# Interleaving the two halves of the stationary operands of a two-block network on one core

## The chip, the cores and the metric
One core of a Trainium2 chip runs the whole program in one launch. The metric is the device time of an execution in microseconds (us), the median of three runs.

## The reference
The input is x, 256 positions by 1024 features, fp32. Two blocks of two layers each follow one another, and every matrix product is wanted at fp32 accuracy:

- First block: a gMLP mixer (1024 to 4096 columns, GELU, a spatial product over positions, 2048 back to 1024), a SwiGLU FFN, then banded attention with relative bias, a second SwiGLU FFN and an RMS norm. The FFNs are 1024 to 2 x 2816 and 2816 back to 1024.
- Second block, twice: a mixer of three branches (a depthwise convolution, causal attention, gated linear attention in chunks of 32) with an output projection of 1024 rows, then an FFN whose up projection passes through a causal convolution of width 3 before the gate.

```python
def _swiglu_ffn(x, g_norm, w_gate_up, w_down):
    h = _rms_norm(x, g_norm)
    gate, up = jnp.split(h @ w_gate_up, 2, axis=-1)
    return (jax.nn.silu(gate) * up) @ w_down
...
        u = causal_depthwise_conv(h @ ffn_w_up[l].astype(h.dtype), ffn_conv_w[l], ffn_conv_b[l])
        x = x + (jax.nn.silu(u[..., :D_FF]) * u[..., D_FF:]) @ ffn_w_down[l].astype(x.dtype)
```

## The kernel before
Every fp32 operand of a large product is split in two fp32r tiles: a high part `hi` (ScalarE copies the value to fp32r) and a remainder `lo` (VectorE subtracts `hi` from the value). A product is then three matmuls: hi x hi, hi x lo and lo x hi. For activations `split2` does this (L232 on ScalarE, L233 on VectorE), for weights the class `Stream`.

`Stream` brings 406 weight pieces of 128 x 1024 from HBM, two to a DMA of 1 MB (issued by SyncE, three raw buffers), in the order in which the program uses them. `_hi` (L105) and `_lo` (L116, or L118 where a row gain is folded in) split a piece into the tiles `wh` and `wl`, 8 buffers each (`LOOK`), or `xh` and `xl`, 4 buffers (`DEFER`), for the last pieces of an FFN's down projection. `pump` is called at points that are written out by hand between the products and does one such step ahead of need; `take` hands pieces over, `release` gives their buffers back. All instructions stand in program order on their engines.

Four forms of product use the pieces. In a matmul, `lhsT` is the stationary operand: a weight load (LDWEIGHTS, 128 columns) puts it into the array before `rhs`, the moving operand, streams through. Each matmul here loads its own.
- `mmA` (L339): position-major; the stationary operand is a 128-position slice of the normalised activations `hT`, the weights move (512 columns).
- `mmB` (L350 to L352): feature-major; the weight piece is stationary in eight parts of 128 columns, `hT` moves (256 positions), three matmuls a part.
- `mmB_wide` (L363, L366): the same with `hT`'s halves side by side, so that `wide` moves 512 columns under the weight's high part and `low` moves 256 under its remainder. The FFNs' up projections use it.
- `down` (L393 to L395): the activations (`ah`, `al`; `uvh`, `uvl` in the gMLP; `yT` in the mixers, which the profile calls hT) are stationary, the weights move (512 columns).

An FFN loops over 22 feature pairs i: two `mmB_wide`, the gating of pair i (`finish`: in the convolution FFNs L634 to L661, with four three-operand VectorE instructions at L651), and `down` for pair i - 3, which takes four matmul groups of three. The pieces that `mmB` and `mmB_wide` take come from `colsB` in the packing code, those of `mmA` from `colsA`, those of `down` from `rowsK`.

Of the kernel before, what the change touches and what calls it, by code (L numbers as in the profile page):

```python
# [9 lines left out]
F32R = mybir.dt.float32r  # L10
# [5 lines left out]
P = 128  # L16
S = 256
D = 1024
KD = D // P
# [3 lines left out]
LOOK = 8  # L23
NBIG = 12
RAW = 3
DEFER = 4
# [21 lines left out]
class Stream:  # L48

    def __init__(self, nc, raw_pool, pool, units):
        self.nc, self.raw_pool, self.pool = nc, raw_pool, pool
        self.units = units
        self.raw = {}
        self.split = {}
        self.index = []
        for u, (src, ext) in enumerate(units):
            for j, e in enumerate(ext):
                self.index.append((u, j, j == len(ext) - 1, e))  # L60
        self.next_dma = 0
        self.nh = 0
        self.nl = 0
        self.used = 0
        self.order = [[i for i, p in enumerate(self.index) if p[3] == e] for e in (False, True)]
        self.ext_pool = None
        self.ext_left = 0
        self.row_gain = {}

    def dma(self, parts=1, between=None):  # L70
        u = self.next_dma
        if u >= len(self.units):
            return
        src, ext = self.units[u]
        t = self.raw_pool.tile([P, 2048], F32, tag="raw", name="raw")
        n = len(ext) * 1024 // parts
        for i in range(parts):
            self.nc.sync.dma_start(t[:, i * n : (i + 1) * n], src[:, i * n : (i + 1) * n])
            if i == 0 and between is not None:
                between()  # L80
        self.raw[u] = t
        self.next_dma += 1
# [4 lines left out]
    def _hi(self):  # L87
        if self.nh >= len(self.index):
            return False
        u, j, last, e = self.index[self.nh]  # L90
        if e:
            if self.ext_pool is None or not self.ext_left:
                return False
            self.ext_left -= 1
            p, a, b, n = self.ext_pool, "xh", "xl", DEFER
        else:
            if self.used >= LOOK:
                return False
            self.used += 1
            p, a, b, n = self.pool, "wh", "wl", LOOK  # L100
        hi = p.tile([P, 1024], F32R, tag=a, name=a, bufs=n)
        lo = p.tile([P, 1024], F32R, tag=b, name=b, bufs=n)
        r = self.raw[u][:, j * 1024 : (j + 1) * 1024]
        g = self.row_gain.get(self.nh)
        self.nc.scalar.activation(hi, r, AF.Copy, scale=1.0 if g is None else g)  # L105
        self.split[self.nh] = (hi, lo)
        self.nh += 1
        return True

    def _lo(self):  # L110
        u, j, last, e = self.index[self.nl]
        hi, lo = self.split[self.nl]
        r = self.raw[u][:, j * 1024 : (j + 1) * 1024]
        g = self.row_gain.get(self.nl)
        if g is None:
            self.nc.vector.tensor_sub(lo, r, hi.bitcast(F32))  # L116
        else:
            self.nc.vector.scalar_tensor_tensor(lo, r, g, hi.bitcast(F32),  # L118
                                                op0=ALU.mult, op1=ALU.subtract)
        self.nl += 1  # L120
        if last:
            del self.raw[u]
            self.dma()
# [27 lines left out]
class Net:  # L151
# [304 lines left out]
    def gmlp(self, start, hT, half_in, warm, rest, rstd):  # L456
        nc = self.nc
        with self.tc.tile_pool(name="gm", bufs=1) as pool:
# [108 lines left out]
            def group(g):  # L567
                if g % 2 == 0:
                    vnorm(g // 2)
                ps = self.mmB2(hT)  # L570
                u = pool.tile([P, 2, S], F32, tag="u", name="u", bufs=2)
                nc.vector.tensor_mul(u, ps, rrow[:, None, :].to_broadcast([P, 2, S]))
                nc.scalar.activation(u, u, AF.Gelu)
                sp = self.mm([P, 2, 2, P], "sp")
                for j in range(2):
                    f = slice((2 * g + j) * P, (2 * g + j + 1) * P)
                    for t in range(2):
                        nc.tensor.matmul(sp[:, j, t, :], lhsT=v[t][:, f], rhs=wsT[:, g, :],  # L578
                                         start=True, stop=True)
                b = brow[:, g * P : (g + 1) * P]  # L580
                vs = pool.tile([P, 4, P], F32, tag="vs", name="vs", bufs=2)
                nc.vector.tensor_add(vs, sp.rearrange("p j t n -> p (j t) n"),
                                     b[:, None, :].to_broadcast([P, 4, P]))
                nc.vector.tensor_mul(u, u, vs.rearrange("p (j t) n -> p j (t n)", j=2))
                uv = tuple(
                    pool.tile([P, 2, S], F32R, tag=n, name=n, bufs=4) for n in ("uvh", "uvl")
                )
                self.split2(uv[0], uv[1], u)
                uvs[g] = uv

# [29 lines left out]
    def ffn(self, hT, fin, next_gains, conv=None, final=False):  # L620
        nc = self.nc
        with self.tc.tile_pool(name="ff", bufs=1) as pool:
# [5 lines left out]
            def finish(i, ps):  # L628


                if isinstance(ps, list):
                    raw = pool.tile([P, 2, S], F32, tag="sum", name="sum", bufs=2)
                    for j in range(2):
                        nc.scalar.activation(raw[:, j, :], ps[j][:, 1, :], AF.Copy)  # L634
                    for j in range(2):
                        nc.vector.tensor_add(raw[:, j, :], ps[j][:, 0, :], raw[:, j, :])  # L636
                    ps = raw
                if conv is None:
                    g, u = ps[:, 0, :], ps[:, 1, :]
                else:  # L640
                    gu = pool.tile([P, 2, S], F32, tag="gu", name="gu", bufs=2)
                    ws3 = []
                    for j in range(2):
                        q = C_FCV + (conv * 44 + j * NPAIR + i) * 4
                        w = [self.prm[:, q + n : q + n + 1] for n in range(4)]
                        nc.scalar.activation(gu[:, j, :], ps[:, j, :], AF.Identity,  # L646
                                             bias=w[3], scale=w[2])
                        ws3.append(w)
                    for d in (1, 2):
                        for j in range(2):  # L650
                            nc.vector.scalar_tensor_tensor(  # L651
                                gu[:, j, d:], ps[:, j, : S - d], ws3[j][2 - d], gu[:, j, d:],
                                op0=ALU.mult, op1=ALU.add,
                            )
                    g, u = gu[:, 0, :], gu[:, 1, :]
                if conv is None:
                    sg = pool.tile([P, S], F32, tag="sg", name="sg", bufs=2)
                else:
                    sg = g
                nc.scalar.activation(sg, g, AF.Silu)  # L660
                nc.vector.tensor_mul(sg, sg, u)  # L661
                act = tuple(
                    pool.tile([P, S], F32R, tag=n, name=n, bufs=7) for n in ("ah", "al")
                )
                self.split2(act[0], act[1], sg)
                acts[i] = act

# [121 lines left out]
    def attention(self, hTs, fin, second, next_gains):  # L789
        nc = self.nc  # L790
        hkv, hq = hTs
        with self.tc.tile_pool(name="at", bufs=1) as pool:
# [35 lines left out]
            def pv(s):  # L828
                pTs = pTss.pop(s)
                po = self.mm([P, S], "po")  # L830
                for j in range(2):
                    for e in range(2):
                        c = slice((2 * s + e) * 64, (2 * s + e + 1) * 64)
                        r = slice(64 * e, 64 * e + 64)
                        nc.tensor.matmul(po[r, j * P :], lhsT=v[j][:, c],  # L835
                                         rhs=pTs[e][:, 2 * j : 2 + j, :], start=j == 0, stop=j == 1)
                act = tuple(
                    pool.tile([P, S], F32R, tag=n, name=n, bufs=8) for n in ("ah", "al")
                )
                self.split2(act[0], act[1], po)  # L840
                acts[s] = act

# [56 lines left out]
    def mixer(self, l, hT, fin, next_gains):  # L899
# [5 lines left out]
        with self.tc.tile_pool(name="mx", bufs=1) as pool:  # L905
# [312 lines left out]
                nc.vector.tensor_scalar(rsc[:, q], ssc[:, q], 4e-6, None, op0=ALU.add)  # L1218
                self.pow(rsc[:, q], rsc[:, q], 4)

            yT = self.new_hT()

            def b_trans():
                ps = self.mm([P, 2, S], "tr")
# [131 lines left out]
    Net(ctx, tc, a, out, units).run()  # L1356


def _pack(inputs):

    import numpy as np
# [6 lines left out]
        return [t[:, i] for i in range(4)]  # L1368

    def colsB(w):  # L1370
        return [w.reshape(KD, P, P).transpose(1, 0, 2).reshape(P, 1024)]

    def rowsK(w):
        return [w[i * P : (i + 1) * P] for i in range(w.shape[0] // P)]
# [2 lines left out]

    def add(name, pieces, ext=()):
        n = len(pieces)
        if n % 2:  # L1380
            pieces = pieces + [pieces[-1]]
        w = np.stack(pieces).reshape(len(pieces) // 2, 2, P, 1024).transpose(0, 2, 1, 3)
        arr[name] = np.ascontiguousarray(w).reshape(len(pieces) // 2, P, 2048)
        for u in range(len(pieces) // 2):
            plan.append((name, u, [i in ext for i in (2 * u, 2 * u + 1) if i < n]))

    w_in, w_out = f["a_w_in"][0], f["a_w_out"][0]
    ps = []
# [113 lines left out]
```

## Time and profile before
| | |
|---|---|
| median of 3 runs | 1240.5 us (1240.06 to 1240.7) |
| the profiled execution: its time, its span | 1240.27 us, 1238.5 us |
| PE busy, share of the span | 1228.8 us, 99% |
| PEld (weight loads) busy | 1055.0 us, 85% |
| DVE (VectorE) busy | 903.5 us, 73% |
| ACT (ScalarE) busy | 715.1 us, 58% |
| HBM traffic | 226 MB, mean 183 GB/s |

How to read it: busy time of an engine is the union of its instructions. Matmuls are pipelined, so a matmul's own duration is longer than the distance from its start to the next one's start; the page's chain of work follows the last instruction back to what released each step. A group's row has its line, engine and operation, out<-in by the program's names, shapes, the count, then busy us, mean ns of one, and the idle time before with what ended it. L12 is line 12 of the kernel.

### The profile page before, as it was taken

Reading aid. Unit: us, or ns where it says so; the run is one execution under the profiler, and the core shown is the slowest. Engines: PE = TensorE matmul, PEld = TensorE weight load, DVE = VectorE, ACT = ScalarE, POOL = GpSimd, SP = SyncE. Lnnn points to the kernel's source line nnn. Section 1 sums busy time; section 2 is a strip of 40 time slices with the busy share of each in tenths; the row PEclk is TensorE's granted clock in tenths of the full one; section 3 lists DMA queues with packets and bytes.
Section 4 is the critical chain, followed back from the end, with each engine's and each line's share of the span. In section 5 each row is a group of like instructions: output and inputs, shape, how many; then the busy total and the mean of one; then the engine's idle time right before and its main releaser. Section 6 shows DMA issues by size and latency. Waiting matters only on the chain.

```text
span 1238.5 us, 18456 instructions
## 1 busy us (share of the span) xinstructions
PE 1228.8 (99%) x7160; PEld 1055.0 (85%) x7160; DVE 903.5 (73%) x1497; ACT 715.1 (58%) x1237; POOL 41.3 (3%) x95
## 2 busy tenths in 40 slices
PE   9999999999999999999999999999999999999997
PEld 7899888888888888888889878888888978888886
DVE  6676676766567757676669867979885977889874
ACT  7644465655456546565546556667663745767653
POOL 1100000000000000000010010000001011000000
PEclk9999999999999999999999999999999999999999
DMA  8854465675444435567524345557542425566720
GB/s 290 307 201 170 153 210 199 209 267 192 148 161 171 163 134 206 183 238 246 184 103 170 120 155 203 171 187 278 198 170 86 164 75 216 182 221 216 252 71 34
DMA packets 34827, 226.14 MB, mean 183 GB/s; under 512 B 4242, under 2 KB 4660, under 8 KB 9140
## 3 DMA queue, kind: packets, MB, share of 16 engines
q1 hardware_dynamic: 34596, 224.97, 51.7%
q8 instruction: 56, 0.92, 0.3%
q14 instruction: 31, 0.25, 0.1%
q10 hardware_dynamic: 144, 0.00, 0.0%
HBM read 223.91 MB, written 1.05 MB: 182 GB/s over the span
## 4 chain that ended last, share of the span: by engine, by line
PE 97%; DVE 2%; ACT 1%; POOL 0%; issue 0%; POOLq 0%; ACTq 0%
PE mm L363 24%; PE mm L339 12%; PE mm L366 12%; PE acc L393 9%; PE acc L395 9%; PE acc L394 9%; PE mm L350 5%; PE mm L351 4%; PE mm L352 4%; PE tr L239 1%; PE sc L746 1%; PE mm L497 1%; PE pt L777 1%; PE sp L578 1%; PE po L835 1%; PE po L1202 0%
## 5 line engine op out<-in xcount | busy, mean ns | idle before, releaser
L116 DVE TENSOR_TENSOR wl<-raw,wh 128x1024 fp32r<-128x1024 f32 x378 | 458.8, 1223 | 201.0 <-ACT wh L105 200.1
L105 ACT ACTIVATE wh<-raw 128x1024 fp32r<-128x1024 f32 x378 | 395.1, 1055 | 246.1 <-PE mm L363 89.5
L363 PE MATMUL mm<-hT,wh 128*128 128x512 f32 x1280 | 452.1, 397 | 0.0
L366 PE MATMUL mm<-hT,wl 128*128 128x256 f32 x1280 | 333.2, 281 | 0.0
L363 PEld LDWEIGHTS mm<-hT,wh 128*128 128x128 f32 x1280 | 235.2, 188 | 46.2
L366 PEld LDWEIGHTS mm<-hT,wl 128*128 128x128 f32 x1280 | 241.6, 189 | 14.2
L339 PE MATMUL mm<-wh,hT 128*128 128x512 f32 (+1 forms) x480 | 149.1, 383 | 0.0
L350 PE MATMUL mm<-hT,wh 128*128 128x256 f32 x448 | 128.9, 288 | 0.0
L351 PE MATMUL mm<-hT,wh 128*128 128x256 f32 x448 | 126.8, 283 | 0.1
L352 PE MATMUL mm<-hT,wl 128*128 128x256 f32 x448 | 126.6, 283 | 0.0
L393 PE MATMUL acc<-wh,ah 128*128 128x512 f32 x320 | 125.6, 393 | 0.0
L395 PE MATMUL acc<-wh,al 128*128 128x512 f32 x320 | 124.5, 389 | 0.0
L394 PE MATMUL acc<-wl,ah 128*128 128x512 f32 x320 | 124.5, 389 | 0.0
L339 PEld LDWEIGHTS mm<-wh,hT 128*128 128x128 f32 x480 | 86.8, 188 | 16.8 <-issue 1.1
L350 PEld LDWEIGHTS mm<-hT,wh 128*128 128x128 f32 x448 | 85.7, 191 | 5.5 <-issue 5.2
L339 PE MATMUL mm<-wl,hT 128*128 128x512 f32 (+1 forms) x240 | 90.2, 381 | 0.0
L351 PEld LDWEIGHTS mm<-hT,wh 128*128 128x128 f32 x448 | 85.8, 192 | 0.7 <-DVE hT L233 0.5
L352 PEld LDWEIGHTS mm<-hT,wl 128*128 128x128 f32 x448 | 85.8, 191 | 0.0
L636 DVE TENSOR_TENSOR sum<-mm,sum 128x256 f32<-128x256 f32 x160 | 66.6, 419 | 15.1 <-ACT sum L634 15.0
L651 DVE SCALAR_TENSOR_TENSOR gu<-sum,prm,gu 128x255 f32<-128x255 f32 (+1 forms) x160 | 72.7, 480 | 5.4 <-ACT gu L646 3.5
L634 ACT ACTIVATE sum<-mm 128x256 f32<-128x256 f32 x160 | 58.8, 369 | 31.1 <-PE mm L363 30.7
L394 PEld LDWEIGHTS acc<-wl,ah 128*128 128x128 f32 x320 | 60.2, 188 | 13.0
(221 smaller groups left out, 1458.5 us busy)
## 6 DMA issues: line engine op xcount, KB each, us to landing
raw<-in_w_ffn SPq DMA_DIRECT2D x66, 1024.0 KB, 4.9
raw<-in_w_up SPq DMA_DIRECT2D x66, 1024.0 KB, 4.9
raw<-in_w_mix SPq DMA_DIRECT2D x30, 1024.0 KB, 4.9
raw<-in_w_gmlp SPq DMA_DIRECT2D x22, 1024.0 KB, 5.1
raw<-in_w_att SPq DMA_DIRECT2D x16, 1024.0 KB, 4.9
raw<-in_w_gmlp SPq DMA_DIRECT2D x4, 512.0 KB, 6.2
bias<-in_rel SPq DMA_DIRECT2D x8, 256.0 KB, 3.9
x<-in_x SPq DMA_DIRECT2D x4, 256.0 KB, 5.4
```

The lines of the kernel that those rows point to most:

```text
L105: self.nc.scalar.activation(hi, r, AF.Copy, scale=1.0 if g is None else g)
L116: self.nc.vector.tensor_sub(lo, r, hi.bitcast(F32))
L339: mm(out, lhsT=hT[a][:, k, ts], rhs=view(b, k), start=(i == 0), stop=(i == 3 * KD - 1))
L350: mm(out, lhsT=vh[:, k, :], rhs=hT[0][:, k, :], start=(k == 0), stop=False)
L351: mm(out, lhsT=vh[:, k, :], rhs=hT[1][:, k, :], start=False, stop=False)
L352: mm(out, lhsT=vl[:, k, :], rhs=hT[0][:, k, :], start=False, stop=(k == KD - 1))
L363: mm(ps, lhsT=vh[:, k, :], rhs=hT[2][:, k], start=(k == 0), stop=(k == KD - 1))
L366: mm(ps[:, 0, :], lhsT=vl[:, k, :], rhs=hT[0][:, k, :], start=False, stop=False)
L393: mm(acc, lhsT=act[0][:, ts], rhs=w[0][:, c], start=(first and i == 0), stop=False)
L394: mm(acc, lhsT=act[0][:, ts], rhs=w[1][:, c], start=False, stop=False)
L395: mm(acc, lhsT=act[1][:, ts], rhs=w[0][:, c], start=False, stop=(last and i == n - 1))
L651: nc.vector.scalar_tensor_tensor(gu[:, j, d:], ps[:, j, : S - d], ws3[j][2 - d], gu[:, j, d:], op0=ALU.mult, op1=ALU.add,)
```

## The change
The high part and the remainder of operands that are loaded as stationary ones now share one tile and alternate element by element: element n of `hi` lies at 2n, element n of `lo` at 2n + 1. That holds for the weight pieces of `mmB` and `mmB_wide` (marked by a class `Stationary` in `colsB`), and for the activations that `down` takes: `ah`/`al` of FFNs and attention, `uvh`/`uvl`, and the mixers' `yT`. Pieces whose weights move (`colsA`, `rowsK`) share one tile too, but as two runs of 1024, one behind the other. A tile of the stream is 2056 elements of which 2048 are used; before, hi and lo were two tiles of 1024. `hT` of the normalised activations stays as it was. Instructions, their order and the DMAs are the same; the access patterns change: ScalarE writes `hi`, VectorE reads `hi` and writes `lo`, and the weight loads read, all at every second element.

```diff
@@ Stream._hi
-            p, a, b, n = self.ext_pool, "xh", "xl", DEFER
+            t = self.ext_pool.tile([P, 2048], F32R, tag="x", name="x", bufs=DEFER)
...
-            p, a, b, n = self.pool, "wh", "wl", LOOK
-        hi = p.tile([P, 1024], F32R, tag=a, name=a, bufs=n)
-        lo = p.tile([P, 1024], F32R, tag=b, name=b, bufs=n)
+            t = self.pool.tile([P, 2056], F32R, tag="w", name="w", bufs=LOOK)[:, :2048]
+        if inter:
+            t = t.rearrange("p (n j) -> p j n", j=2)
+        else:
+            t = t.rearrange("p (j n) -> p j n", j=2)
+        hi, lo = t[:, 0, :], t[:, 1, :]
@@ gmlp
-                uv = tuple(
-                    pool.tile([P, 2, S], F32R, tag=n, name=n, bufs=4) for n in ("uvh", "uvl")
-                )
+                uv = pool.tile([P, 2, S, 2], F32R, tag="uv", name="uv", bufs=4)
+                uv = (uv[:, :, :, 0], uv[:, :, :, 1])
@@ ffn (attention the same, with 8 buffers)
-                act = tuple(
-                    pool.tile([P, S], F32R, tag=n, name=n, bufs=7) for n in ("ah", "al")
-                )
+                act = pool.tile([P, S, 2], F32R, tag="a", name="a", bufs=7)
+                act = (act[:, :, 0], act[:, :, 1])
@@ mixer
-            yT = self.new_hT()
+            yT = self.hpool.tile([P, KD, S, 2], F32R, tag="hT", name="yT")
+            yT = (yT[:, :, :, 0], yT[:, :, :, 1])
@@ packing
+class Stationary(tuple):
+    def __new__(cls, piece):
+        return super().__new__(cls, (piece,))
...
-        return [w.reshape(KD, P, P).transpose(1, 0, 2).reshape(P, 1024)]
+        return [Stationary(w.reshape(KD, P, P).transpose(1, 0, 2).reshape(P, 1024))]
```

## Rows read from the trace of the kernel before
**Rows 1.** The page: busy us and share, granted clock in 40 slices, chain by engine.
```profile
PE 1228.8 (99%) x7160; PEld 1055.0 (85%) x7160; DVE 903.5 (73%) x1497; ACT 715.1 (58%) x1237; POOL 41.3 (3%) x95
...
PEclk9999999999999999999999999999999999999999
...
PE 97%; DVE 2%; ACT 1%; POOL 0%; issue 0%; POOLq 0%; ACTq 0%
```
**Rows 2.** Waits of PE, then of ACT: us in total, times, longest us.
```profile
PE warm L423 <- POOL ident masks.py:199: 1.4, 1, 1.4
...
PE acc L393 <- ACT ah L232: 0.2, 1, 0.2
...
ACT wh L105 <- PE mm L363: 89.5, 76, 1.8
```
**Rows 3.** Groups by line and shape, whole span.
```profile
L363 PE MATMUL mm<-hT,wh 128*128 128x512 f32 x1280 | 452.1, 397 | 0.0
...
L366 PE MATMUL mm<-hT,wl 128*128 128x256 f32 x1280 | 333.2, 281 | 0.0
...
L350 PE MATMUL mm<-hT,wh 128*128 128x256 f32 x448 | 128.9, 288 | 0.0
...
L393 PE MATMUL acc<-wh,ah 128*128 128x512 f32 x320 | 125.6, 393 | 0.0
...
L393 PE MATMUL acc<-wh,uvh 128*128 128x512 f32 x64 | 25.7, 402 | 0.0
L393 PE MATMUL acc<-wh,hT 128*128 128x512 f32 x64 | 25.5, 398 | 0.0
...
L393 PE MATMUL acc<-xh,ah 128*128 128x512 f32 x60 | 24.1, 402 | 0.2 <-ACT ah L232 0.2
```
**Rows 4.** Timeline of PE in an FFN, 301.2 to 306.3: start us, us.
```profile
301.21 0.40 PE L393 MATMUL acc<-wh,ah 128*128 128x512 f32 x1
...
303.93 0.39 PE L363 MATMUL mm<-hT,wh 128*128 128x512 f32 x1
...
304.27 0.40 PE L363 MATMUL mm<-hT,wh 128*128 128x512 f32 x1
...
304.98 0.40 PE L363 MATMUL mm<-hT,wh 128*128 128x512 f32 x1
305.22 0.28 PE L366 MATMUL mm<-hT,wl 128*128 128x256 f32 x1
305.33 0.40 PE L363 MATMUL mm<-hT,wh 128*128 128x512 f32 x1
...
306.04 0.40 PE L363 MATMUL mm<-hT,wh 128*128 128x512 f32 x1
```
**Rows 5.** Timeline of PE, then of PEld, in a mixer, 694.9 to 699.0.
```profile
694.90 0.28 PE L350 MATMUL mm<-hT,wh 128*128 128x256 f32 x1
...
697.66 0.28 PE L352 MATMUL mm<-hT,wl 128*128 128x256 f32 x1
...
697.68 1.34 PEld L777 LDWEIGHTS pt<-ident,z 128*128 128x128 f32 x12
698.98 0.19 PEld L339 LDWEIGHTS mm<-wh,hT 128*128 128x128 f32 x1
```
**Rows 6.** The chain in order of time, gMLP: start us, us, what.
```profile
59.88 0.89 PE sp L578 x8
```
**Rows 7.** Windows, convolution FFNs: stretch, us, busy of PE, PEld, DVE, ACT, POOL.
```profile
752.00:925.00 173.00, 173.00 (x915) 147.95 (x914) 146.20 (x242) 116.07 (x197) 0.86 (x2) 1.00 0.61 209
1050.00:1225.00 175.00, 174.79 (x922) 149.07 (x921) 142.04 (x240) 110.49 (x190) 0.00 (x0) 1.00 0.49 171
```
**Rows 8.** Groups by line and shape on DVE, whole span.
```profile
L116 DVE TENSOR_TENSOR wl<-raw,wh 128x1024 fp32r<-128x1024 f32 x378 | 458.8, 1223 | 201.0 <-ACT wh L105 200.1
...
L651 DVE SCALAR_TENSOR_TENSOR gu<-sum,prm,gu 128x255 f32<-128x255 f32 x80 | 37.4, 478 | 3.6 <-ACT gu L646 3.5
...
L233 DVE TENSOR_TENSOR al<-sg,ah 128x256 fp32r<-128x256 f32 x44 | 18.5, 420 | 0.3 <-ACT ah L232 0.3
```

More of the change, by code (lines that the diff above doesn't have):

```diff
@@ L57, in __init__ @@
         self.index = []
-        for u, (src, ext) in enumerate(units):
+        for u, (src, ext, kinds) in enumerate(units):
             for j, e in enumerate(ext):
-                self.index.append((u, j, j == len(ext) - 1, e))
+                self.index.append((u, j, j == len(ext) - 1, e, kinds[j]))
         self.next_dma = 0
@@ L73, in dma @@
             return
-        src, ext = self.units[u]
+        src, ext, _ = self.units[u]
         t = self.raw_pool.tile([P, 2048], F32, tag="raw", name="raw")
@@ L89, in _hi @@
             return False
-        u, j, last, e = self.index[self.nh]
+        u, j, last, e, inter = self.index[self.nh]
         if e:
@@ L110, in _lo @@
     def _lo(self):
-        u, j, last, e = self.index[self.nl]
+        u, j, last, e, _ = self.index[self.nl]
         hi, lo = self.split[self.nl]
@@ L836, in pv @@
                                          rhs=pTs[e][:, 2 * j : 2 + j, :], start=j == 0, stop=j == 1)
-                act = tuple(
-                    pool.tile([P, S], F32R, tag=n, name=n, bufs=8) for n in ("ah", "al")
-                )
+                act = pool.tile([P, S, 2], F32R, tag="a", name="a", bufs=8)
+                act = (act[:, :, 0], act[:, :, 1])
                 self.split2(act[0], act[1], po)
@@ L1379, in add @@
         n = len(pieces)
+        kinds = [isinstance(p, Stationary) for p in pieces]
+        pieces = [p[0] if k else p for p, k in zip(pieces, kinds)]
         if n % 2:
@@ L1384, in add @@
         for u in range(len(pieces) // 2):
-            plan.append((name, u, [i in ext for i in (2 * u, 2 * u + 1) if i < n]))
+            plan.append((name, u, [i in ext for i in (2 * u, 2 * u + 1) if i < n], kinds[2 * u : 2 * u + 2]))
     w_in, w_out = f["a_w_in"][0], f["a_w_out"][0]
@@ L1496 @@
     out = nc.dram_tensor("out", (1, S, D), F32, kind="ExternalOutput").ap()
-    units = [(a[name][u], ext) for name, u, ext in plan]
+    units = [(a[name][u], ext, kinds) for name, u, ext, kinds in plan]
     with _tile.TileContext(nc) as tc:
```

## Prediction, made before the changed kernel was run
> **What bounds the kernel now.** Read the page's busy times and its chain first. [...] Then the waits of PE: the longest total is 1.4 us, at the start, and a down projection waits for an activation once, for 0.2 us [rows 2]. So no feeding engine sets the time. What can change it is the time from one matmul's start to the next one's, and the diff changes how the operand that every matmul loads first is laid out. That interval is not the duration in the groups (397 ns for a 512-wide matmul [rows 3]), since matmuls overlap; it is read from the starts in the timeline.
>
> [...]
> - Down projection (L393 to L395, 512 wide): from 301.21 to 303.93 us lie twelve intervals, 2.72 us, 226.7 ns each, 13.3 over the stream [rows 4].
> - Wide pair (L363 with 512 columns, L366 with 256): from 304.98 to 306.04 lie three pairs, 1.06 us, 353.3 ns a pair, 33.3 over the 320.0 of its two streams [rows 4].
> - Narrow triple (L350 to L352, 256 wide): from 694.90 to 697.66 lie 23 intervals, 2.76 us, 120.0 ns each, 13.3 over [rows 5].
>
> So there is time between matmuls that is neither stream nor wait. It is not one constant: the first wide pair after a down projection takes 340 ns (303.93 to 304.27), the settled ones 353 [rows 4], with the same operations on the same kinds of tiles. I read this as two read streams (the load of the next stationary operand, the moving columns of the current one) that get in each other's way by an amount that depends on how they fall against each other. That reading is argued; the rows only show that the amount varies.
>
> How much there is: 1280 pairs at 33.3 ns are 42.7 us; 448 triples, 1344 matmuls, at 13.3 are 17.9; the L393 groups of 512 columns are 320 + 64 + 64 + 60 = 508 [rows 3], as many stand in L394 and L395, and 1524 at 13.3 are 20.3. Together **81 us** over the streams, all in matmuls whose stationary operand the diff lays out anew. The other product, mmA (L339), loads hT, which stays as it is.
>
> **The change part by part.** *The loads.* Each still takes 128 columns of 128 rows, but its elements lie 8 bytes apart instead of 4. No row shows such a load, so bounds from both sides. For the gain, the rows with the closest loads: the transposes load every 108 ns (from 697.68 to 698.98 twelve loads [rows 5]), and the gMLP's spatial matmuls (L578), which load without transposing, start every 111 ns (0.89 us for 8 [rows 6]), that is 4.6 ns over a stream of 106.7. If every stationary operand came down to 4.6 over, a pair gains 24.1 ns, the others 8.7: 1280 x 24.1 + 1344 x 8.7 + 1524 x 8.7 = 30.8 + 11.7 + 13.3 = 56 us. By the transposes' 1.7 it would be 72 us; at nothing left, 81. For the loss: a load is covered by the interval of the matmul before it, 120 ns in the triple and 0.11 us behind the narrow half of a pair [rows 4]; its own pace is 108. So a load that slows by a few per cent costs nothing, and one that doubles (216 ns) raises each interval behind a 256-wide stream to 216: 96 x 1344 + 106 x 1280 = 265 us. I take the gain of 56, by the row that loads in the same manner. The reason for the sign: a contiguous load fetches its bytes at half the pace at which the moving stream does (128 columns in 108 ns, against 256 in 106.7), so the two slide past each other; at 8 bytes a column they advance alike, and an offset found once should last.
>
> *The writers.* ACT's L105 and L232 write, and DVE's L116 and L233 read one and write one operand, at every second element. 216 of the 406 weight pieces are concerned (gmlp 16, four FFNs 40 each, attention 16, mixers 12 each). The instruction counts don't change, and hT's writers are left alone but for the mixers' yT. Below, the price is nothing: these run at one element at a time, 1223 ns for 1024 [rows 8]. Above, the dearest elementwise row: L651, 478 ns for 255 columns, 1.87 ns a column against L116's 1.19 [rows 8], so 0.70 us more a piece and 0.17 more a 256-column activation. I take nothing, since nothing says that a strided operand is like L651. What covers it is DVE's idle time, and that differs by stage: in the loops of the two convolution FFNs DVE is busy 288.2 of 348.0 us, 83% [rows 7].
>
> [...]
>
> *One tile instead of two, padded by 8 elements.* The slot of a weight piece comes free when its last reader is done; hi's last reader and lo's are at most one matmul apart (120 to 227 ns), and ACT waits for such slots already (89.5 us in 76 waits behind L363 alone [rows 2]) without PE waiting. Nothing. Should hi's readers now also wait for the lo written beside it (420 ns [rows 8]), that shows only where a down projection follows its activation at once, in the tails: some 2 us in all, not counted. DMAs, queues and their order don't change.
>
> *The sum.* A loop of a convolution FFN has 16 pairs and 12 down matmuls: 16 x 353.3 + 12 x 226.7 = 8.37 us, DVE at 83% of it 6.93. Its gain is 16 x 24.1 + 12 x 8.7 = 0.49 us, which leaves 7.88 and DVE at 88%. With 348 / 8.37 = 41.6 loops that is 20 us, and I count half of it, because at 88% ACT and DVE, which wait for each other, will let PE wait at times. 56 - 10 = 46. From the profiled execution's 1240.3 us (the median of the runs is 1240.5): **1194 us**.
>
> **Rivals.** *One: DVE becomes the bound in the convolution FFNs.* Two strided pieces and an activation a loop, 2 x 0.70 + 0.17 = 1.57 us, put DVE at 8.50: the 20 us are lost, 0.13 x 41.6 = 5 more are paid, and the other stages keep 36: 1240 + 5 - 36 = 1209. If half of DVE's present idle time (0.72 of 1.44 us a loop, spent waiting for ACT) stays, a loop takes 9.22, 35 us more in all, and the time is 1239. If PE gains nothing as well, the two ends are 1245 and 1275. [...] For it speaks DVE's 83%; against it that L116 already runs at one element at a time.
>
> *Two: the stride makes no difference to TensorE* and its 13 ns are a fixed cost of switching the stationary operand. The exact repeat of 226.7 and 120.0, both 13.3 over, speaks for it; 340 against 353 for the same pair against it. 1240.
>
> *Three, the other side: the loads get slower.* Place: every matmul behind a 256-wide stream, in 1344 + 1280 cases; it decides from a load of 110 to 120 ns on. At 135 ns (a quarter more) the triples pay 15 x 1344 = 20 us and the pairs 25 x 1280 = 32: 1292. At double the time it is 1505; if not the load but the mutual hindrance doubles, 1240 + 81 = 1321. For it: twice as many bytes are spanned by each load. Against it: the load's own 108 ns look like one column at a time, which a stride need not touch.
>
> **How the numbers follow.** Forecast 0.47 (its own range 1168, by the transposes' floor, to 1215); rival one with a gain on PE 0.15 (1209 to 1239, of which 0.02 falls within 0.2%), without one 0.09 (1245 to 1275); rival two 0.14; rival three 0.15. Faster by over 0.2% (about what a measurement of this kernel can tell from no change): 0.47 + 0.13 = 0.60. Same 0.14 + 0.02 = 0.16. Slower 0.09 + 0.15 = 0.24. The range goes from 1168 to 1262, which leaves out rival three and the upper part of rival one without a gain, 0.18 in all.
>
> **What would show it.** In the profile after: wide pairs at about 329 ns, triples at 111, down projections at 218, mmA at its old interval. L116 at 1223 ns for the strided pieces; a second, longer form of it would be rival one, with PE waiting behind DVE in L651 or L363. Loads of over 188 ns in their records and triples over 120 would be rival three. Unchanged intervals would be rival two. Most likely to make me wrong: that the hindrance is not a matter of pace, or that only some of the eight buffers, which the pad shifts by 8 elements each, fall well.

## The result, and the profile after

| | before | after |
|---|---|---|
| median of 4 runs each, us | 1240.34 | 1251.66 |
| lowest to highest, us | 1240.06 to 1240.70 | 1251.58 to 1251.73 |
| ratio, 95% interval | | 1.0091 [1.0074, 1.0109] |
| profiled execution: span, us | 1238.5 | 1249.8 |

The change makes the kernel 11.3 us slower. That lies inside the range that was given (1168 to 1262) and on the other side of the forecast, which was a gain of 46 us. The range was wide enough to take in two rivals, and that the time lies in it is luck.

The page of after, busy time and chain, and the first waits of PE (us in total, times, longest us), answer to [rows 1, 2]:

```profile
PE 1240.3 (99%) x7160; PEld 1078.0 (86%) x7160; DVE 905.9 (72%) x1497; ACT 734.1 (59%) x1237; POOL 42.3 (3%) x95
...
PEclk9999999999999999999999999999999999999999
...
PE 97%; DVE 1%; ACT 1%; issue 0%; POOL 0%; POOLq 0%; ACTq 0%
```
```profile
PE warm L427 <- POOL ident masks.py:199: 1.4, 1, 1.4
PE mm L501 <- DVE w L120: 0.8, 2, 0.4
```

The reader is to see that nothing new is waited for. The 0.8 us behind a weight's remainder stood in the kernel before too. PE is busy 11.5 us longer in a span that is 11.3 us longer, the chain is still PE's for 97%, and the granted clock is 0.999 of full speed, as before. So no feeding engine took the time; it lies between one matmul's start and the next.

The groups of after, by line and shape (busy us, mean ns of one), answer to [rows 3, 8]. Lines are four higher than before: L363 is now L367, L116 is L120, L339 is L343.

```profile
L120 DVE TENSOR_TENSOR w<-raw,w 128x1024 fp32r<-128x1024 f32 x378 | 459.1, 1224 | 210.7 <-ACT w L109 209.1
L109 ACT ACTIVATE w<-raw 128x1024 fp32r<-128x1024 f32 x378 | 413.8, 1105 | 236.8 <-PE mm L367 87.7 <-PE acc L399 64.9 <-PE mm L356 36.1
...
L367 PEld LDWEIGHTS mm<-hT,w 128*128 128x128 f32 x1280 | 244.4, 196 | 39.1
```

The last two of them in the kernel before:

```profile
L105 ACT ACTIVATE wh<-raw 128x1024 fp32r<-128x1024 f32 x378 | 395.1, 1055 | 246.1 <-PE mm L363 89.5 <-PE acc L395 62.5 <-PE mm L351 46.0
...
L363 PEld LDWEIGHTS mm<-hT,wh 128*128 128x128 f32 x1280 | 235.2, 188 | 46.2
```

DVE takes 1224 ns for a weight's remainder (1223 before) and 420 for an activation's (420 before), so the 8-byte step costs it nothing. ACT's high parts rise from a mean of 1055 to 1105 ns, with about half of them written at the step, and ACT is busy 59%. A load of a pair is recorded at 196 ns instead of 188.

The timeline of PE in an FFN (start us, duration us), two loops one after the other, answers to [rows 4]:

```profile
304.38 0.39 PE L397 MATMUL acc<-w,a 128*128 128x512 f32 x1
...
307.15 0.39 PE L367 MATMUL mm<-hT,w 128*128 128x512 f32 x1
...
307.85 0.39 PE L367 MATMUL mm<-hT,w 128*128 128x512 f32 x1
...
308.90 0.39 PE L367 MATMUL mm<-hT,w 128*128 128x512 f32 x1
...
312.76 0.39 PE L397 MATMUL acc<-w,a 128*128 128x512 f32 x1
...
315.57 0.40 PE L367 MATMUL mm<-hT,w 128*128 128x512 f32 x1
```

The twelve intervals of the down projection take 2.77 us in the first loop and 2.81 in the next, about 231 and 234 ns each, against 226.7 in [rows 4]. Three pairs take 1.05 us, 350 ns a pair against 353. So the pairs are hardly changed, the down projection is slower, and no longer by one number. Over the loops that follow each other the means of twelve are 233.5, 233.8, 232.7, 233.1, 234.7, 233.4, 230.2, 230.8, and then the same eight again: they follow the eight weight buffers, which the pad sets 32 bytes apart.

mmA pays too, though its stationary operand was left alone. This is its first long stretch in the chain in order of time (start us, us, what), in the kernel before and then in after:

```profile
20.67 33.01 PE mm L339 x144
```
```profile
20.82 33.61 PE mm L343 x144
```

33.61 instead of 33.01 us for 144 matmuls, 4.2 ns more each. mmA's moving columns are the contiguous weight pieces, and these lie in the same padded ring of buffers.

From the starts in the two traces every interval can be taken. The table gives the mean over the stream: from start to next start, less 213.3 ns at 512 columns and 106.7 at 256. These two are estimates: 106.7 is the difference of the 226.7 ns at 512 columns and the 120.0 at 256 in [rows 4, 5], and 213.3 is twice that. Intervals more than 40 ns over, which hold waits and changes of sequence, are left out of it (16.2 us in all before, 15.9 after); the counts are those of after.

| product, columns | matmuls | before, ns | after, ns | change, us |
|---|---|---|---|---|
| down projection, 512 | 1490 | 14.20 | 19.35 | +7.7 |
| mmA, 512 | 571 | 14.78 | 19.06 | +2.5 |
| pair, narrow half, 256 | 1280 | 10.58 | 11.75 | +1.5 |
| triple, 256 | 1301 | 13.14 | 13.61 | +0.6 |
| pair, wide half, 512 | 1276 | 21.36 | 20.72 | -0.8 |

The sum is 11.5 us. (Five more of mmA's intervals are counted after than before; they are 0.1 of its 2.5.) The same measure, "over" for short, is used for all runs below.

### The profile page after: what moved, and what is told of

It is laid out like the page before. It is cut to its first block, busy times and chain, and to the rows that moved or that the text cites. A ratio compares the mean times of both kernels' runs of the same rounds, so it can differ in the third digit from the quotient of the medians.

```text
span 1249.8 us, 18447 instructions
## 1 busy us (share of the span) xinstructions
PE 1240.3 (99%) x7160; PEld 1078.0 (86%) x7160; DVE 905.9 (72%) x1497; ACT 734.1 (59%) x1237; POOL 42.3 (3%) x95
## 3 DMA queue, kind: packets, MB, share of 16 engines
HBM read 223.91 MB, written 1.05 MB: 180 GB/s over the span
## 4 chain that ended last, share of the span: by engine, by line
PE 97%; DVE 1%; ACT 1%; issue 0%; POOL 0%; POOLq 0%; ACTq 0%
PE mm L367 24%; PE mm L343 12%; PE mm L370 12%; PE acc L397 9%; PE acc L399 9%; PE acc L398 9%; PE mm L354 5%; PE mm L355 4%; PE mm L356 4%; PE tr L243 1%; PE sc L748 1%; PE mm L501 1%; PE pt L779 1%; PE sp L582 1%; PE po L837 1%; PE po L1203 0%
## 5 line engine op out<-in xcount | busy, mean ns | idle before, releaser
L120 DVE TENSOR_TENSOR w<-raw,w 128x1024 fp32r<-128x1024 f32 x378 | 459.1, 1224 | 210.7 <-ACT w L109 209.1
L109 ACT ACTIVATE w<-raw 128x1024 fp32r<-128x1024 f32 x378 | 413.8, 1105 | 236.8 <-PE mm L367 87.7
L367 PE MATMUL mm<-hT,w 128*128 128x512 f32 x1280 | 452.2, 396 | 0.0
L370 PE MATMUL mm<-hT,w 128*128 128x256 f32 x1280 | 334.2, 281 | 0.0
L367 PEld LDWEIGHTS mm<-hT,w 128*128 128x128 f32 x1280 | 244.4, 196 | 39.1
L370 PEld LDWEIGHTS mm<-hT,w 128*128 128x128 f32 x1280 | 250.7, 196 | 11.9
L343 PE MATMUL mm<-w,hT 128*128 128x512 f32 (+1 forms) x720 | 168.9, 386 | 0.0
L343 PEld LDWEIGHTS mm<-w,hT 128*128 128x128 f32 x720 | 126.4, 188 | 27.8 <-issue 2.2
L354 PE MATMUL mm<-hT,w 128*128 128x256 f32 x448 | 129.3, 289 | 0.0
L355 PE MATMUL mm<-hT,w 128*128 128x256 f32 x448 | 127.0, 284 | 0.1
L356 PE MATMUL mm<-hT,w 128*128 128x256 f32 x448 | 126.8, 283 | 0.0
L397 PE MATMUL acc<-w,a 128*128 128x512 f32 x320 | 126.7, 396 | 0.0
L399 PE MATMUL acc<-w,a 128*128 128x512 f32 x320 | 126.3, 395 | 0.0
L398 PE MATMUL acc<-w,a 128*128 128x512 f32 x320 | 126.2, 394 | 0.0
L354 PEld LDWEIGHTS mm<-hT,w 128*128 128x128 f32 x448 | 87.9, 196 | 5.5 <-issue 5.2
L355 PEld LDWEIGHTS mm<-hT,w 128*128 128x128 f32 x448 | 87.9, 196 | 0.7 <-DVE hT L237 0.5
L356 PEld LDWEIGHTS mm<-hT,w 128*128 128x128 f32 x448 | 87.9, 196 | 0.0
L639 DVE TENSOR_TENSOR sum<-mm,sum 128x256 f32<-128x256 f32 x160 | 66.9, 419 | 15.9 <-ACT sum L637 15.6
L399 PEld LDWEIGHTS acc<-w,a 128*128 128x128 f32 x320 | 62.5, 195 | 12.0
L398 PEld LDWEIGHTS acc<-w,a 128*128 128x128 f32 x320 | 62.4, 195 | 11.7
```

The costliest lines, as they stand in the source:

```text
L343: mm(out, lhsT=hT[a][:, k, ts], rhs=view(b, k), start=(i == 0), stop=(i == 3 * KD - 1))
L354: mm(out, lhsT=vh[:, k, :], rhs=hT[0][:, k, :], start=(k == 0), stop=False)
L355: mm(out, lhsT=vh[:, k, :], rhs=hT[1][:, k, :], start=False, stop=False)
L356: mm(out, lhsT=vl[:, k, :], rhs=hT[0][:, k, :], start=False, stop=(k == KD - 1))
L367: mm(ps, lhsT=vh[:, k, :], rhs=hT[2][:, k], start=(k == 0), stop=(k == KD - 1))
L370: mm(ps[:, 0, :], lhsT=vl[:, k, :], rhs=hT[0][:, k, :], start=False, stop=False)
```

## Experiments

**Which part of the change costs.** Theory 1: the pad puts the weights of the eight buffers at offsets that meet the other stream less well. Its rival: a load at a step of 8 bytes is dearer by itself. Five kernels take the change apart. (The theories are numbered as in the expectations; there is none with the number 2.)

*e1_no_pad*: all is interleaved, the pad is gone.
```
-            t = self.pool.tile([P, 2056], F32R, tag="w", name="w", bufs=LOOK)[:, :2048]
+            t = self.pool.tile([P, 2048], F32R, tag="w", name="w", bufs=LOOK)
```


> The changed kernel with weight tiles of 2048 elements instead of 2056, so that all eight start at the same offset within 256 bytes; everything stays interleaved. Theory 1 (the pad puts the moving weights of down and mmA at offsets 32 bytes apart, and their settled interval of 226.7 ns is lost): down back to about 13 to 14 ns over its stream from 19.4, mmA from 19.1 to about 15, time about 1241 us. Rival (the strided loads, 196 ns instead of 188, cost it): intervals as after the change, 1251 us.

*e2_one_tile*: one tile for both parts, as two contiguous runs; no pad, nothing interleaved.
```
-            t = self.pool.tile([P, 2056], ...)[:, :2048]
-        if inter:
+            t = self.pool.tile([P, 2048], ...)
+        if False:
...
-                act = pool.tile([P, S, 2], F32R, tag="a", name="a", bufs=7)
-                act = (act[:, :, 0], act[:, :, 1])
+                act = tuple(pool.tile([P, S], F32R, tag=n, name=n, bufs=7) for n in ("ah", "al"))
```


> Only the joint tile of hi and lo, as two runs of 1024, no pad and nothing interleaved. Theory 1 and the rival alike: 1240 us, as before the change. If it is near 1250 instead, what costs is that hi and lo of a piece lie 4096 bytes apart or share a slot.

*e3_pad_only*: e2 with the tile of 2056.

> The joint tile with the pad of 8 elements, as two runs, nothing interleaved. Theory 1: down about 19 ns over its stream, mmA about 19, time 1249 to 1252 us, with loads at 188 ns. Rival: 1240 us.

*e4_weights_only*: the change with the activations' lines (act, uv, yT) as they were before.

> The changed kernel with the activations of down back in separate contiguous tiles; weight pieces interleaved and padded as in the change. Theory 1: 1249 to 1252 us, down as slow as after the change although its loads are contiguous again. Rival: most of the loss sits in down, so about 1242 to 1243 us.

*e5_acts_only*: e2 with only those activations interleaved; no pad.

> Only the activations of down interleaved; weight pieces in one tile as two runs, no pad. Theory 3 (what costs is the position of the load's reads against the moving reads: a stride of 8 bytes spoils a settled pair of aligned contiguous operands, a pad of 32 bytes does so too): down about 21 ns over its stream as without the pad but all interleaved, nothing else moves, so 1240.3 + 1489 x 7.2 ns = 1251 us. Rival (the strided loads of the weight pieces cost as well): about 1246 us, the rest of the loss being theirs.

Measured, with e8_weights_no_pad, which came later (below) and completes the scheme:

| run | interleaved | pad | us | ratio [95%] | down | mmA | triple | pair (wide + narrow) |
|---|---|---|---|---|---|---|---|---|
| before | nothing | no | 1240.34 | | 14.20 | 14.78 | 13.14 | 21.36 + 10.58 |
| e2 | nothing, one tile | no | 1240.31 | 0.9999 [0.9991, 1.0008] | 14.16 | 14.83 | 13.14 | 21.38 + 10.56 |
| e3 | nothing | yes | 1244.86 | 1.0038 [1.0025, 1.0050] | 18.22 | 18.94 | 11.68 | 18.78 + 11.69 |
| e5 | activations | no | 1248.33 | 1.0065 [1.0048, 1.0082] | 19.67 | 14.73 | 13.10 | 21.71 + 10.55 |
| e8 | weights | no | 1240.64 | 1.0004 [0.9995, 1.0013] | 14.02 | 14.61 | 13.32 | 20.10 + 11.37 |
| e1 | both | no | 1252.23 | 1.0096 [1.0081, 1.0112] | 21.43 | 14.86 | 13.32 | 21.70 + 10.98 |
| e4 | weights | yes | 1251.10 | 1.0087 [1.0073, 1.0101] | 18.67 | 19.03 | 13.59 | 20.77 + 11.88 |
| after | both | yes | 1251.66 | 1.0091 [1.0074, 1.0109] | 19.35 | 19.06 | 13.61 | 20.72 + 11.75 |

What a run costs is taken against the runs of the kernel before that were made beside it (1240.16 to 1240.30 us).

Theory 1 had asked for about 1241 us in e1, where 1252.23 came out, its rival's side; for 1249 to 1252 in e3, where 1244.86 lies between it and its rival's 1240; and for the same in e4, where it holds (1251.10). In e5 Theory 3, which is told below, had asked for 1251 us and its rival for 1246; 1248.33 lies between the two. So Theory 1 falls as the whole cause and holds for a part.

The joint tile costs nothing (e2). The pad alone costs 4.6 us (e3): mmA and the down projections lose, triples and pairs gain. Interleaved activations alone cost about 8 us (e5), nearly all of it in the down projections, which load them: this is the largest single part, and between e2 and e5 nothing differs but how these activations lie: at the step, with `lo` 4 bytes behind `hi`. Without the pad mmA is back at 14.86 (e1), so what mmA pays is the pad's. In the whole change the pad gives back elsewhere what it takes there: without it the time is 1252.23 us, with it 1251.66. The parts don't add: interleaved weights cost 0.4 us without the pad (e8) and 6.2 with it (e3 to e4), most of which is what the pad had given to triples and pairs.

The timeline of PE shows the down projection in one loop, twelve intervals from its first row to the next, in e1 and then in e3:

```profile
303.94 0.40 PE L397 MATMUL acc<-w,a 128*128 128x512 f32 x1
...
306.76 0.40 PE L367 MATMUL mm<-hT,w 128*128 128x512 f32 x1
```
```profile
303.33 0.39 PE L397 MATMUL acc<-w,ah 128*128 128x512 f32 x1
...
306.11 0.40 PE L367 MATMUL mm<-hT,w 128*128 128x512 f32 x1
```

235.0 ns each with the step alone, 231.7 with the pad alone, against 226.7: either is enough to leave the better pattern.

**The interval by itself.** Theory 3: the interval depends on where the load's reads fall against the moving stream's, that is on the offset of the two operands (within 256 bytes) and on the step. Two kernels of matmuls alone measure it.

*m1_pace*: 36 equal matmuls a line, with the stationary operand shifted and stepped.
```
+for _ in range(36): mm(ps, lhsT=L(0), rhs=R(0, 512), start=True, stop=True)      # L39
+for _ in range(36): mm(ps, lhsT=L(1), rhs=R(0, 512), start=True, stop=True)      # L40, 4 bytes on
...
+for _ in range(36): mm(ps, lhsT=L(0, 2), rhs=R(0, 512), start=True, stop=True)   # L52, step 8 bytes
```


> A kernel with matmuls alone: 78 rows of 36 equal matmuls, every one with its own load of 128 columns, 512 or 256 moving columns, the stationary operand contiguous, at every second or at every fourth element, and its start or the moving operand's start shifted by 4 to 512 bytes. It computes nothing of the reference. Theory 3: contiguous and aligned settles at 13.3 ns over the stream; with a stride of two the interval over the stream depends on the shift and differs from 13.3 by several ns in either direction. Rival (a strided load costs a fixed amount): the same excess for all shifts of one stride, larger with the stride. If loads at every fourth element take over 120 ns at 256 columns, the load's own pace is the limit there.

It ran once, 590.73 us. The timeline of PE (start us, us; the interval is the difference of two successive lines' starts over 36) begins with the contiguous operand, shifted by 0 and 4 bytes (L39, L40), by 128 and 256 (L45, L46):

```profile
34.83 8.33 PE L39 MATMUL ps<-mv,st 128*128 128x512 f32 x36
43.00 8.53 PE L40 MATMUL ps<-mv,st 128*128 128x512 f32 x36
51.37 8.47 PE L41 MATMUL ps<-mv,st 128*128 128x512 f32 x36
...
84.86 8.53 PE L45 MATMUL ps<-mv,st 128*128 128x512 f32 x36
93.23 8.33 PE L46 MATMUL ps<-mv,st 128*128 128x512 f32 x36
101.39 8.32 PE L47 MATMUL ps<-mv,st 128*128 128x512 f32 x36
...
142.91 8.57 PE L52 MATMUL ps<-mv,st 128*128 128x512 f32 x36
151.31 8.55 PE L53 MATMUL ps<-mv,st 128*128 128x512 f32 x36
...
362.42 4.46 PE L78 MATMUL ps<-mv,st 128*128 128x256 f32 x36
366.72 4.42 PE L79 MATMUL ps<-mv,st 128*128 128x256 f32 x36
...
409.29 4.24 PE L89 MATMUL ps<-mv,st 128*128 128x256 f32 x36
413.37 4.43 PE L90 MATMUL ps<-mv,st 128*128 128x256 f32 x36
417.64 4.48 PE L91 MATMUL ps<-mv,st 128*128 128x256 f32 x36
421.95 4.48 PE L92 MATMUL ps<-mv,st 128*128 128x256 f32 x36
...
473.81 8.56 PE L104 MATMUL ps<-mv,st 128*128 128x256 f32 x36
482.20 8.56 PE L105 MATMUL ps<-mv,st 128*128 128x256 f32 x36
```

At 512 columns: 226.9 unshifted (L39), 232.5 at 4 bytes (L40) and at 128 (L45), 226.7 at 256 (L46) and at 512. So the pattern of no shift comes back at 256 bytes; all shifts of 4 to 128 bytes gave 230.6 to 233.3, and a shift of the moving operand by 16 to 128 bytes 228.6 to 233.6. At a step of 8 bytes it is 233.3 unshifted (L52), and 230.3 to 233.6 over all thirteen offsets. At 256 columns the picture is another: 119.4 unshifted (L78), 113.3 with the moving operand 64 bytes on (L89), 119.7 at a step of 8 bytes (L91). At a step of 16 bytes the interval behind a 256-wide stream is 233.1 (L104), with the load recorded at 328 ns; by the expectation's measure, 120 ns, the load is the limit there. At 8 bytes (196 ns) the interval is 119.7.

Theory 3 is half met. The interval does hang on the offset, and a step adds no fixed amount; but with the 8-byte step it differs from the unshifted contiguous one upward only at 512 columns, and by 1.4 ns at most either way at 256 (118.6 to 120.8), where Theory 3 had several ns in either direction. A 512-wide matmul at that step takes 3.6 to 6.9 ns more than at the best contiguous offset, about what a contiguous operand takes at the other offsets. An 8-byte step that finds a lasting good offset, as the prediction had it, is in none of these rows.

*m2_forms*: the same in the kernel's three orders, each line one order at one offset. (The kernel takes the last of every eight pairs the other way round, narrow half first; m2 leaves that out.)
```
+for q, w, r in list(triple(vw(0, 1))) * 3: mm(q, lhsT=w, rhs=r, start=True, stop=True)    # L60
+for q, w, r in list(triple(vw(16, 1))) * 3: mm(q, lhsT=w, rhs=r, start=True, stop=True)   # L64, 64 bytes on
```


> A kernel with matmuls alone, in the kernel's own three orders: triples, wide pairs and down groups, each with its own load, the stationary operand contiguous with its start shifted by 0 to 240 bytes, or at every second element. It computes nothing of the reference. Theory 3 (position of the two read streams, not stride as such): unshifted and contiguous gives the intervals of the kernel before (triples 120 ns, pairs 353, down 226.7); triples settle at 113 to 118 for some shift; pairs, as the padded kernel's buffers suggest, at 347 to 350; down is never under 226.7. With every second element no shift is better than 120 and 226.7. Rival (strided loads have a price of their own): triples and pairs at every second element are slower than unshifted contiguous ones by as much as down is, about 5 ns a matmul.

It ran once, 520.8 us. The chain in order of time (start us, us, what); triples at 0 and 64 bytes and at a step of 8 (L60, L64, L80), pairs at 0, 32 and 8 bytes and at the step (L83, L85, L99, L103), down projections at 0 and 32 bytes and at the step (L106, L107, L111):

```profile
35.57 8.63 PE ps L60 x72
...
69.73 8.16 PE ps L64 x72
...
205.49 8.64 PE ps L80 x72
...
231.41 8.48 PE ps L83 x48
...
248.22 8.32 PE ps L85 x48
...
365.79 8.32 PE ps L99 x48
...
399.23 8.33 PE ps L103 x48
...
424.42 10.89 PE ps L106 x48
435.31 11.19 PE ps L107 x48
...
479.85 11.19 PE ps L111 x48
```

A triple's matmul takes 119.9 ns at offset 0, 113.3 at 64 bytes, 120.0 at the step. A pair takes 353.3 at 0 and 346.7 to 347 at 8, at 32 bytes and at the step (351 at the other two offsets of the step). A down projection's takes 226.9 at 0 and 233.1 at 32 bytes and at the step. That is as Theory 3 forecast, which said nothing of pairs at the step. Its rival, 5 ns a matmul more at the step in triples and pairs, falls. So the operands of the kernel before stood at the best offset measured here for the down projection, and not for triples and pairs. The 6.6 ns of the pairs are the only gain of over 1 ns that the step brought in matmuls alone, where the prediction had 24.1.

**Is it of use in place, and has the step a price of its own?**

*e7_shift*: contiguous operands as in e3, but every buffer at a multiple of 256 bytes, and the stationary pieces of triples 64 bytes, those of pairs 32 bytes into it. To make room there are six activation buffers instead of seven, and two softmax tiles share a tag.
```
+            t = self.pool.tile([P, 2112], F32R, tag="w", name="w", bufs=LOOK)
+            t = t[:, inter : inter + 2048]
+        t = t.rearrange("p (j n) -> p j n", j=2)
...
+TRIPLE, PAIR = 16, 8      # elements
```


> The kernel before, contiguous halves in one tile, with only the weight pieces that are loaded as stationary shifted: by 64 bytes for the triples, by 32 bytes for the wide pairs; the weights that move in mmA and down stay at multiples of 256 bytes. (To make room, six activation buffers instead of seven and one tag for two small softmax tiles.) Theory 3 (position decides): triples at 113.3 ns instead of 120.0, pairs at 346.7 instead of 353.3, down and mmA unchanged, 1344 x 6.7 + 1280 x 6.6 = 17 us, so about 1223 us. If position matters only in a stream of matmuls alone, 1240 us.

Measured: 1239.00 us, 0.9989 [0.9980, 0.9998], where 1223 were forecast. Triples are at 8.74 over, which is 4.4 ns gained and not 6.7: they settle at 113 to 114 ns in some stretches and at 118 in others. The pairs are at 21.25 + 11.65, not at 26.7 together: in an FFN 240, 121, 229, 117 ns keep returning in the first eight of a loop and 232, 118, 238, 119 in the next eight, about 353 a pair. The down projections, whose operands did not move, went from 14.20 to 16.08. The timeline of PE shows how, one down projection and the pairs behind it:

```profile
301.29 0.40 PE L395 MATMUL acc<-w,ah 128*128 128x512 f32 x1
...
303.14 0.39 PE L397 MATMUL acc<-w,al 128*128 128x512 f32 x1
...
304.06 0.39 PE L365 MATMUL mm<-hT,w 128*128 128x512 f32 x1
...
305.12 0.39 PE L365 MATMUL mm<-hT,w 128*128 128x512 f32 x1
```

Its first eight intervals take 1.85 us, 231 ns each, and from the ninth it is back at 227, but for the last, at 235 ns; in the kernel before it is there from the second. Three pairs take 1.06 us. So offset and step are not all: how a sequence runs depends on what ran before it as well. This is Theory 4. The kernel before shows it too, in one line and at one offset. Its pairs at 353 ns stand behind down projections [rows 4]; here are three that stand behind transposes:

```profile
169.59 0.82 PE L694 MATMUL tr<-ident,gr 128*128 128x128 f32 x6
...
170.94 0.39 PE L363 MATMUL mm<-hT,wh 128*128 128x512 f32 x1
...
171.98 0.40 PE L363 MATMUL mm<-hT,wh 128*128 128x512 f32 x1
```

They take 1.04 us, 347 ns each. From the third to the seventh pair of such a stretch the mean is 346.5 ns in all four FFNs, and 354.0 in the 76 stretches behind mmA or a down projection. Why the pairs of e7 don't run at m2's 347 is not shown: in e7 they settle at 353 behind down projections, mmA and transposes alike, so a down projection ahead is not what decides it there.

*e8_weights_no_pad*: only the weights interleaved, no pad (e1 with the activations as before). The expectation's 2624 loads of narrow matmuls are 1344 of triples and 1280 of pairs.

> Only the stationary weight pieces interleaved, no pad, activations contiguous. Theory 3: in the kernel's own orders, triples stay at 120 ns, pairs near 353 as in the run without the pad, down and mmA as before: 1240 to 1242 us, although 2624 + 1280 - 1280 = 2624 narrow and 1280 wide matmuls then load at 196 ns. Rival (a strided load costs of itself): 5 ns for each of these 3904 matmuls, 1260 us.

Measured: 1240.64 us, 1.0004 [0.9995, 1.0013], with loads at 195 to 196 ns in their records. The rival falls: for triples (13.32 over, 13.14 in e2) and pairs (31.5 against 31.9) an 8-byte step has no price that shows. That doesn't carry over to the down projections, where the same step costs 5.5 ns a matmul (e5 against e2).

*e9_triple_64*: e7 with `TRIPLE, PAIR = 16, 0`.

> As the run with both shifts, but the wide pairs' weights unshifted: only the triples' weight pieces lie 64 bytes off. Theory 4 (a sequence settles in one of several patterns, which one depends on offset, stride and on the phase in which it is entered, and hands a phase on to the next): triples at 113 to 118 as with both shifts, 8.7 ns over their stream; pairs 32 over, down 14.2 and mmA as in the kernel before, since they are entered as there: 1240.2 - 1344 x 4.4 ns = 1234 us. Rival (down lost 1.9 ns for another reason than the pairs ahead of it): down stays at 16 and the time is 1237 us.

Measured: 1234.97 us, 0.9957 [0.9945, 0.9970]; triples 9.04, pairs 21.31 + 10.58, down 14.09, mmA 14.83. This is Theory 4's number within 1 us, with all that was left in place unmoved. Since nothing but the pairs' offset differs from e7, it is the pairs ahead that had cost the down projections their 1.9 ns.

*e10_pair_8*: e7 with `TRIPLE, PAIR = 16, 2`.

> As the run with both shifts, with 8 bytes instead of 32 for the wide pairs. By the matmul-only kernel, which gave 346.7 ns for 8 bytes as for 32: pairs 26 to 27 over, 1224 to 1230 us. Theory 4: which pattern is reached is decided at the entry from down, as with 32 bytes (33 over); 1232 to 1241 us, and each loop of an FFN repeats the same intervals.

Measured: 1229.55 us, 0.9914 [0.9901, 0.9928], 10.7 us under the kernel before. Triples are at 8.74, pairs at 18.03 + 10.20, down at 13.85, mmA at 15.02. The timeline of PE in an FFN, as in [rows 4]:

```profile
299.45 0.39 PE L395 MATMUL acc<-w,ah 128*128 128x512 f32 x1
...
302.17 0.40 PE L365 MATMUL mm<-hT,w 128*128 128x512 f32 x1
...
303.22 0.40 PE L365 MATMUL mm<-hT,w 128*128 128x512 f32 x1
...
304.26 0.39 PE L365 MATMUL mm<-hT,w 128*128 128x512 f32 x1
```

The down projection keeps its 226.7 ns (2.72 us for twelve), and three pairs take 1.04 us; over all pairs the mean is 348.2 ns instead of 351.9. Theory 4's forecast, from 1232 us on, missed by 2.5 us: the entry from the down projection did not hold these pairs at 353. The forecast by m2, 1224 to 1230, has the time, though the pairs stayed at 28.2 over and did not reach 26 to 27. It is the fastest of the kernels run.

## Why the prediction was wrong

One row of the kernel before, from its groups by line and shape, is needed below (128 partitions by 128 columns):

```profile
L578 PE MATMUL sp<-wsT,v 128*128 128x128 f32 x64 | 8.4, 275 | 0.0
```

- **Where the time can move: right.** No wait of PE grew by more than 0.2 us, and the whole change lies in intervals, 11.5 us by the table of forms.
- **The excess is no fixed cost: right.** Rival two would leave all intervals; they moved between 113.3 and 120.0 (m1, m2) with the offset alone.
- **The writers cost no time: right.** DVE takes 1223 to 1224 ns a piece. ACT takes 50 ns more in the mean, which was not foreseen and is covered by 41% of idle time. Rival one asked for 0.70 us a piece; at the 8-byte step DVE's 1224 ns for 1024 columns are 1.20 a column, 1.19 before. With the stationary load behind a 256-wide stream the interval is 119.7 ns at 8 bytes and 119.4 contiguous, and at 16 bytes it is 233.1 (m1).
- **No load becomes the limit: right.** Of the signs named for rival three the faint ones came: 196 ns in the record instead of 188, and triples at 13.61 instead of 13.14 over. They are worth 0.6 us, not the 52 of that rival, and e8 shows no price of the step in triples and pairs.
- **The step that failed** is the sign of the loads' term: "at 8 bytes a column they advance alike, and an offset found once should last". From it came a gain of 56 us. The pairs, put at a gain of 30.8 us, lost 0.7; the triples, put at 11.7, lost 0.6; the down projections, put at 13.3, lost 7.7. The 226.7 was not a chance collision that any other layout would loosen: it was the best of the patterns measured at that width, and interleaving the activations alone lost it (e5, about 8 us). That the excess varies left its sign open, and the prediction settled it by an argument on pace that no row bore.
- **The size of that term failed too, by a misread row.** The 4.6 ns were 111 ns less 106.7, which the prediction takes for 256 columns. But L578 moves 128, by its row above: half of that is 53.3 ns, and it stands 58 over. The transposes, from which the 1.7 came, move 128 columns too. So neither row showed a 256-wide or 512-wide matmul that comes nearer to its stream.
- **The streams under that term, 213.3 and 106.7 ns, are shown by no run.** 106.7 is what the interval grows by from 256 columns to 512 in [rows 4, 5]; that a matmul can come down to it, as the 81 us assume, is not shown. The shortest settled intervals measured are 226.7 ns at 512 columns (m1), 113.3 at 256 (m1, m2) and 346.5 to 346.7 for a pair (the kernel before behind transposes, m2). Against these the kernel before had 1280 x 6.6 + 1344 x 6.7 ns = 17 us to gain, in pairs and triples, and none in the down projections.
- **The pad was costed at nothing, as a matter of buffers coming free. That failed too:** it moves the operands against each other. Alone it costs 4.6 us (e3). In the change 2.5 us of it lie in mmA, a product which the prediction left out since its stationary operand was unchanged; but the down projections, with the step, run better with the pad than without (19.35 against 21.43), and in sum the pad there costs nothing (e1). "That only some of the eight buffers, which the pad shifts by 8 elements each, fall well" was named as a way to be wrong. The means that repeat every eight loops show that the buffers differ, but without the pad the time is no better, so this is not what turned the sign.
- **Rival one's range without a gain, 1245 to 1275, holds the time by luck:** its cause, a slower DVE, did not come.
- **The 10 us set aside for DVE** were not asked for, since there was no gain for DVE to hold back.

What stays open: why the pattern comes back at 256 bytes, why the step loses the 226.7 ns of the down projection at every offset tried, and why a run of pairs keeps 353 ns at one offset and takes 347 at the next. Which pattern a sequence enters was not predicted by any theory here, only measured (e7 against e10). Which part of the layout costs how much is shown; that two read streams get in each other's way is argued from offsets and steps, and no run looked inside.

## What to carry to other kernels

Where TensorE sets the time and waits for nothing, take the interval from start to start, by the form of product, and compare it with the shortest that matmuls alone reach at that width; the duration in the groups hides it (393 ns for L393, where the interval is 226.7). Before laying an operand out anew, measure the new layout's interval in matmuls alone and in the kernel's order, at the offsets that the buffers will have, moving operand included; a pad of a few bytes is a change of layout for every product that reads that ring. A row of another width is no price: a variation that has been seen can go either way.

## What the runs showed of the hardware

- The interval of settled 512-wide matmuls with a load each is 226.7 ns when stationary and moving operands stand as the tiles begin, or the stationary one 256 or 512 bytes on, and 228.6 to 233.6 at the other offsets and at an 8-byte step (m1). At 256 columns the best offset is another: 113.3 with the moving operand 64 bytes on (m1) or the triples' stationary one 64 or 192 bytes on (m2), 115.7 to 120.0 at the other contiguous offsets, 64 bytes of the stationary operand in m1 (117.8) among them. In the kernel triples at 64 bytes ran at 113 to 118 (e7).
- Behind 256-wide streams a matmul with a stationary load at an 8-byte step takes 118.6 to 120.8 ns (m1), against 113.3 to 120.0 with a contiguous one; at a 16-byte step it takes 233.1 to 236.4. At 512 columns the 8-byte step keeps the matmul at 230.3 or more.
- The interval of a sequence depends on what ran ahead of it: in the kernel before the same pairs take 346.5 ns behind transposes and 354.0 behind mmA or a down projection. A down projection whose operands did not move needs eight intervals of 231 ns to come to 227 when the pairs ahead stand at 32 bytes (e7), and one when they stand at 0.
- 64 bytes for one kind of weights and 8 for the other are worth 10.7 us of 1240 (e10), and TensorE, DVE and ACT execute as many instructions as before (7160, 1497, 1237).
